# Moving TensorE's tiles in SBUF: operands on a line of 128 bytes, weights 64 bytes behind one

## The chip, the cores and the metric

The kernel runs on one core of a Trainium2 chip. The metric is the device time of one execution in microseconds (us), the median of several runs. SBUF is the on-chip memory that the engines read; a tile has 128 partitions, and a position in this document is a byte within a partition. "At 32" means 32 bytes behind a multiple of 128.

## The reference

One encoder layer on 1,024 tokens of 1,024 channels, all in float32:

```
h = x + 0.5 * SwiGLU_1(RMSNorm(x))                      # 1024 -> 2*2816 -> 1024
proj = RMSNorm(h) @ w_in                                # q, k, v, g_ret, p_pool, two gates (7 * 1024)
ret = retention(rotary(q), rotary(k), v)                # 4 heads of 256, chunks of 64, decay per head
ret = headnorm(ret) * silu(g_ret)
pool_out = (trailing means of windows 2/4/8/16 - token) @ pool_w * pool_scale
merged = sigmoid(gate0) * (ret @ w_ret_up) + sigmoid(gate1) * (pool_out @ w_pool_up)
h = h + merged @ w_out
h = h + 0.5 * SwiGLU_2(RMSNorm(h))
return RMSNorm(h)
```

Nearly all work is in the matrix products.

## The kernel before

Activations lie with channels on partitions and tokens along the row. Every float32 operand of a product is split into a high and a low float32r part (`split`, L150, and `split_scaled`, L154: ScalarE writes the high part, VectorE the rest), and `mm3` (L169) multiplies three times: high by high, high by low, low by high (L171 to L173). TensorE's instruction for one multiplication is a load of 128x128 weights and a stream of up to 512 moving columns; the load for the next one runs beside the stream.

The large products use Strassen's scheme (`strassen`, L415: seven products of blocks in place of eight), and some pairs of groups a second level of it with 256 columns (`common`, L521; it puts the blocks made by `blocks`, L337, into tiles of tags `tl` and `t4`). VectorE forms the sums and differences, and the low parts, of weights and operands. `values` (L1159) computes v with the roles swapped: the activations are the stationary operand and tiles of `wt` move. In the retention units (`Unit`, L1360) both operands are tiles of `mv`, except the masked scores `sm` (stationary, tag `t4`) and the running state (moving, tag `t4`). The end of the last stage (`turned`, L948) multiplies two operand tiles. `spread` (L224) multiplies by `ones_r`.

The order is written out by hand. `Flow.run` (L64) takes a list of steps, each a preparation (loads, weights) and a body (products); the preparation of a step comes four steps (`LOOK`) ahead of its body, and after each body one or two pieces of put-off VectorE and ScalarE work are taken from a queue. One step of a Strassen group is 4 x 3 multiplications. Nearly all DMAs are issued by SyncE (`load`, L133).

Tiles come from two pools in SBUF, `cp` and then `sb`. Within a pool tags are laid out in the order of their first request, each with its number of buffers, sizes rounded up to 32 bytes. Adding them up from the first free byte, 1,152 (itself a multiple of 128), gives:

| tiles | bytes of one x buffers | begins before (behind a multiple of 128) | after |
|---|---|---|---|
| vec, neg, cst | 256, 256, 1344 | 0, 0, 0 | same |
| warm, zero, ones_r | 32, 1024, 512 | 64, 96, 96 | same |
| `line` (new) | 32 | - | 96 |
| t4 (activations, results; sm, state), raw (weights as loaded) | 4096 x 9, 4096 x 4 | 96 | 0 |
| ss | 32 x 2 | 96 | 0 |
| wt (split weights) | 4096 x 5 | 32 | 64 |
| `between` (new) | 64 | - | 64 |
| mv (split operands), tl (loaded or spilled tiles) | 4096 x 28, 4096 x 4 | 32 | 0 |
| c2 (half tiles: sums, differences) | 2048 x 8 | 32 | 0 |

All slices that TensorE reads begin at multiples of 512 bytes within these tiles. Small tiles (roots, sums, edges) follow behind c2.

Of the kernel before, what the change touches and what calls it, by code (L numbers as in the profile page):

```python
# [10 lines left out]
F32 = mybir.dt.float32  # L11
F32R = mybir.dt.float32r
# [5 lines left out]
P = 128  # L18
# [31 lines left out]
N_MV, N_T4, N_RAW, N_WT, N_TL, N_C2 = 28, 9, 4, 5, 4, 8  # L50
# [39 lines left out]
def block_kernel(ctx: ExitStack, tc, x, x_tok, vecs, f1_in, f1_out, w_in, w_v, pool_w, w_ret, w_pool, w_o,  # L90
# [10 lines left out]
    cp = ctx.enter_context(tc.tile_pool(name="cp", bufs=1))  # L101
    sb = ctx.enter_context(tc.tile_pool(name="sb", bufs=1))
# [4 lines left out]
    def mv(name):  # L107
        return sb.tile([P, 2, H], F32R, tag="mv", bufs=N_MV, name=name)

    def wt(name):  # L110
        return sb.tile([P, 2, 4, P], F32R, tag="wt", bufs=N_WT, name=name)


    def raw(name):
# [48 lines left out]
    def weights(src, name):  # L163
        w = wt(name)
        n = src.shape[-1] // P
        split(flat(w, 0, n), flat(w, 1, n), src)
        return w
# [25 lines left out]
            mm(b, zero[:, :P], zero, start=True, stop=True)  # L193
    ident, ones = cst[:, C_ID : C_ID + P], cst[:, C_ONE : C_ONE + P]
    ones_r = cp.tile([P, P], F32R, name="ones_r")


    def inverse_root(sums, n, name):
# [1649 lines left out]
```

## Time and profile before

| | |
|---|---|
| time, median of 3 runs | 2164.43 us (2164.16 to 2165.67) |
| span of the profiled execution, first to last instruction | 2160.9 us |
| granted TensorE clock | 0.999 |
| TensorE busy with multiplications | 2148.0 us, 10,668 of them |
| VectorE busy | 1870.0 us |
| ScalarE busy | 1088.9 us |
| DMA | 320.92 MB, mean 149 GB/s |

The profiled execution has no time of its own beside its span; the median of the runs is 3.5 us above it. In the profile, "PE" is TensorE's multiplication, "PEld" its load of weights, "DVE" VectorE, "ACT" ScalarE, "SP" SyncE. A row of the timeline gives the start in us from the span's beginning, the length, engine, source line, operation, and written<-read tiles with their shape. Multiplications overlap in the records (a length of 0.39 us where the next starts much earlier), so the pace is read from the distance between starts.

### The profile page before, as it was taken

To read this page: it belongs to the slowest core of one execution; us is meant where nothing else is said; L and a number is where in the kernel's file an instruction comes from. 1 tells how busy PE (TensorE), PEld (TensorE's weight loads), DVE (VectorE), ACT (ScalarE), POOL (GpSimd) and SP (SyncE) were. 2 spreads that over 40 slices of the span, in tenths; PEclk is the share of its full clock that TensorE was granted. 3 is DMA by queue.
4 is the path that set the end of the run, shared out by engine and by line. 5 is a ranking of instruction groups with operands and counts; after the bars stand their busy time and mean duration, and the time that the engine had idled before them with its cause. 6 is when DMAs were issued, how large, how long until landed. Compare 5 with 4: busy or idle time off the path is not lost.

```text
span 2160.9 us, 29697 instructions
## 1 busy us (share of the span) xinstructions
PE 2148.0 (99%) x10668; PEld 1816.9 (84%) x10668; DVE 1870.0 (87%) x3300; ACT 1088.9 (50%) x2047; POOL 0.2 (0%) x4
## 2 busy tenths in 40 slices
PE   9999999999999999999999999999999999999998
PEld 7888888888888888888888898887888888888887
DVE  8799899998788798899767877899999989999784
ACT  8544444545656444444426754446644444455463
POOL 0000000000000000000000000000000000000000
PEclk9999999999999999999999999999999999999999
DMA  7232323596323333333485567624133232359532
GB/s 261 69 129 104 101 93 127 165 339 207 122 93 107 109 127 108 118 107 119 153 268 191 167 224 256 218 97 160 65 117 103 98 107 99 118 185 334 178 122 78
DMA packets 117828, 320.92 MB, mean 149 GB/s; under 512 B 12976, under 2 KB 17200, under 8 KB 117680
## 3 DMA queue, kind: packets, MB, share of 16 engines
q1 hardware_dynamic: 117104, 317.97, 43.4%
q8 instruction: 83, 1.36, 0.3%
q10 hardware_dynamic: 576, 1.05, 0.1%
q14 instruction: 65, 0.53, 0.1%
HBM read 228.27 MB, written 90.70 MB: 148 GB/s over the span
## 4 chain that ended last, share of the span: by engine, by line
PE 90%; DVE 7%; ACT 1%; issue 1%; DMA 1%; SPq 0%; ACTq 0%; DVEq 0%
PE c_b L171 2%; PE c_b L173 2%; PE c_b L172 2%; PE a_b L173 2%; PE a_b L171 2%; PE a_b L172 2%; PE c_e L173 2%; PE c_e L171 2%; PE c_e L172 2%; PE a_e L173 2%; PE a_e L171 1%; PE a_e L172 1%; PE bp6b L172 1%; PE bp6b L173 1%; PE bp6b L171 1%; PE c_a L172 1%
## 5 line engine op out<-in xcount | busy, mean ns | idle before, releaser
L172 PE MATMUL c_b<-n3T,c_wS 128*128 128x512 f32 x176 | 68.5, 389 | 0.0
L173 PE MATMUL c_b<-n3T,c_wS 128*128 128x512 f32 x176 | 68.5, 389 | 0.0
L171 PE MATMUL c_b<-n3T,c_wS 128*128 128x512 f32 x176 | 68.2, 390 | 0.0
L171 PE MATMUL a_b<-n1T,a_wS 128*128 128x512 f32 x168 | 65.5, 390 | 0.0
L172 PE MATMUL a_b<-n1T,a_wS 128*128 128x512 f32 x168 | 65.4, 389 | 0.0
L173 PE MATMUL a_b<-n1T,a_wS 128*128 128x512 f32 x168 | 65.4, 389 | 0.0
L173 PE MATMUL a_a<-n1R,a_wL 128*128 128x512 f32 x120 | 46.7, 390 | 0.8 <-DVE a_wL L152 0.8
L171 PE MATMUL a_a<-n1R,a_wL 128*128 128x512 f32 x120 | 46.8, 390 | 0.0
L172 PE MATMUL a_a<-n1R,a_wL 128*128 128x512 f32 x120 | 46.7, 389 | 0.0
L172 PE MATMUL c_a<-n3R,c_wL 128*128 128x512 f32 x112 | 43.7, 390 | 0.0
L171 PE MATMUL c_a<-n3R,c_wL 128*128 128x512 f32 x112 | 43.6, 389 | 0.0
L173 PE MATMUL c_a<-n3R,c_wL 128*128 128x512 f32 x112 | 43.6, 389 | 0.0
L173 PEld LDWEIGHTS c_b<-n3T,c_wS 128*128 128x128 f32 x176 | 33.0, 188 | 6.9
L171 PEld LDWEIGHTS c_b<-n3T,c_wS 128*128 128x128 f32 x176 | 33.0, 188 | 6.9
L172 PEld LDWEIGHTS c_b<-n3T,c_wS 128*128 128x128 f32 x176 | 33.0, 188 | 6.8
L171 PEld LDWEIGHTS a_b<-n1T,a_wS 128*128 128x128 f32 x168 | 31.5, 188 | 6.8 <-ACT a_v L471 0.3
L173 PEld LDWEIGHTS a_b<-n1T,a_wS 128*128 128x128 f32 x168 | 31.5, 188 | 6.6
L172 PEld LDWEIGHTS a_b<-n1T,a_wS 128*128 128x128 f32 x168 | 31.5, 188 | 6.5
L173 PE MATMUL c_e<-n3T,c_wS 128*128 128x512 f32 x88 | 35.1, 399 | 0.4 <-DVE c_wS L152 0.4
L171 PE MATMUL c_e<-n3T,c_wS 128*128 128x512 f32 x88 | 34.5, 393 | 0.0
L172 PE MATMUL c_e<-n3T,c_wS 128*128 128x512 f32 x88 | 34.4, 391 | 0.0
L173 PE MATMUL a_e<-n1T,a_wS 128*128 128x512 f32 x84 | 33.4, 398 | 0.9 <-DVE a_wS L152 0.9
(3058 smaller groups left out, 8076.2 us busy)
## 6 DMA issues: line engine op xcount, KB each, us to landing
c_ra<-in_f_in SPq DMA_DIRECT2D x22, 512.0 KB, 3.6
c_rb<-in_f_in SPq DMA_DIRECT2D x22, 512.0 KB, 4.1
a_ra<-in_f_in SPq DMA_DIRECT2D x21, 512.0 KB, 3.6
a_rb<-in_f_in SPq DMA_DIRECT2D x21, 512.0 KB, 4.4
t<-au SPq DMA_DIRECT2D x11, 512.0 KB, 2.6
b<-ag SPq DMA_DIRECT2D x11, 512.0 KB, 2.7
r<-au SPq DMA_DIRECT2D x11, 512.0 KB, 3.6
br<-r SPq DMA_DIRECT2D x11, 512.0 KB, 5.4
```

What stands on the lines that cost most here:

```text
L171: mm(dst, w[0], m[0], start=start, stop=False, skip_group_check=True)
L172: mm(dst, w[0], m[1], start=False, stop=False, skip_group_check=True)
L173: mm(dst, w[1], m[0], start=False, stop=stop, skip_group_check=True)
```

## The change

Two tiles are allocated that no instruction reads or writes. `line`, 32 bytes, stands at the end of the pool `cp`. `between`, 64 bytes, is requested once, right behind the first weights' tile, so that it lies behind the five buffers of `wt`. Everything allocated behind them moves up, as the table shows. No instruction, order, buffer count or shape changes.

```diff
+    between = []
+
     def wt(name):
-        return sb.tile([P, 2, 4, P], F32R, tag="wt", bufs=N_WT, name=name)
+
+        w = sb.tile([P, 2, 4, P], F32R, tag="wt", bufs=N_WT, name=name)
+        if not between:
+            between.append(sb.tile([P, 16], F32, tag="between", bufs=1, name="between"))
+        return w
...
     ones_r = cp.tile([P, P], F32R, name="ones_r")
+    cp.tile([P, 8], F32, name="line")
```

## Prediction

> **What bounds the kernel now.** I read the head of the page first (the span and the engines' shares), then TensorE's waits, then the chain of waits by engine.
>
> ```profile
> span 2160.9 us, 29697 instructions
> PE 2148.0 (99%) x10668; PEld 1816.9 (84%) x10668; DVE 1870.0 (87%) x3300; ACT 1088.9 (50%) x2047; POOL 0.2 (0%) x4
> PE set L193 <- DVE zero L188: 1.2, 1, 1.2
> PE a_e L173 <- DVE a_wS L152: 0.9, 2, 0.5
> PE 90%; DVE 7%; ACT 1%; issue 1%; DMA 1%; SPq 0%; ACTq 0%; DVEq 0%
> ```
>
> TensorE has 10,668 multiplications and is busy for 99%. Its longest waits are 1.2 and 0.9 us in total, and 90% of the chain is TensorE's own work. So the kernel is paced by how far apart two multiplications start, with VectorE (87%) close behind. A busy share says nothing of whether that distance is as short as it could be, so I measured it in the timeline, over stretches in which nothing waits. First, 512 columns, nine steps apart:
>
> ```profile
> 499.75 0.39 PE L171 MATMUL bp6b<-bp7m,bp7w 128*128 128x512 f32 x1
> ...
> 501.79 0.39 PE L171 MATMUL bp1a<-bp2m,bp2w 128*128 128x512 f32 x1
> ```
>
> 2.04 / 9 = 0.2267 us. Then 256 columns, where weights and moving operand both begin 32 bytes behind a line of 128 (13 steps), and 256 columns with the weights `sm` 96 behind and the moving `v` 32 behind (18 steps):
>
> ```profile
> 155.77 0.28 PE L171 MATMUL a_x<-n1R,a_wx 128*128 128x256 f32 x1
> ...
> 157.33 0.28 PE L172 MATMUL a_b<-n1R,a_wx 128*128 128x256 f32 x1
> 1183.66 0.28 PE L171 MATMUL ob<-v,sm 128*128 128x256 f32 x1
> ...
> 1185.70 0.28 PE L171 MATMUL xb<-state,q 128*128 128x256 f32 x1
> ```
>
> 1.56 / 13 = 0.1200 us and 2.04 / 18 = 0.1133 us. The same shape, the same engine, no waits, and 6% apart: the one thing that I find to differ systematically is where the tiles begin. That is the row on which this prediction rests.
>
> **What the change moves.** It adds no instruction, no wait and no transfer: two tiles that nobody writes, 32 and 64 bytes wide, shift what is allocated behind them. Positions are worked out from tile sizes and order of allocation (the section on the kernel has the table). Moving operands go from 32 (some from 96) to 0; the weights' tiles from 32 to 64, which is half a line from the moving operands. Tiles that VectorE, ScalarE and the DMA queues use go from 96 or 32 to 0.
>
> **Step 1: what a position costs.** 0.1200 − 0.1133 = 0.0067 us looks like a unit: 0.1200 is 18 of it, 0.1133 is 17, and 0.2267 is 34. Sixteen fp32 columns are 64 bytes, so 256 columns are 16 pieces of 64 bytes and 512 are 32. Beyond the pieces there are 2 units in 256 columns with equal positions, 1 with positions half a line apart, and 2 in 512 columns with equal positions. My reading: one unit because the operand begins inside a piece (32 bytes behind a 64-byte boundary) and touches one piece more, and one because the weights being loaded collide with it in the same half of a line. Both would go: 32 units = 0.2133 us for 512 columns, 0.1067 for 256. No row shows an fp32 product with the moving operand at 0 and the weights at 64; the bounds are 0.2133 (no unit left) and, above, the 0.230 that the last rival quotes. I take 0.2133, because the only steady rows half a line apart, those of 0.1133, lie on its side.
>
> A page bears on the size. The Trainium skill ("TensorE: Matmul & The Clock Gate", the section on 56 ns against 53.3 ns) gives 215.7 ns between warm multiplications of 512 columns, a fixed 2.5 ns above the bare columns. No row here shows it; by it some 19 us of the gain below would be lost (an estimate) and the sum would come to about 2084 us.
>
> For 256 columns the load of the weights may become the limit. Transposes, 128 columns with a load each, run at the load's pace:
>
> ```profile
> 2065.06 0.87 PE n4t L1674 x8
> ```
>
> 0.87 / 8 = 0.109 us, so I take 0.109 and not 0.1067.
>
> **Step 2: how many of each.** Counted over the program's multiplications, which match the 10,668 of the page's row one for one:
> - 512 columns, 32/32 before, half a line apart after (activations against weights' tiles, and the value projection where the roles are swapped): 7,896 × (0.2267 − 0.2133) = 105.3 us.
> - 512 columns, both in operand tiles and both at 0 after (the last stage's turned products): 132; one unit each, 0.9 us.
> - 256 columns, 32/32 before, half a line apart after: 1,578 × (0.1200 − 0.109) = 17.4 us.
> - 256 columns with the moving operand in a tile of tag t4, apart before and after: 228 × (0.1133 − 0.109) = 1.0 us.
> - 256 columns, both at 0 after (scores, state updates): 240, one unit each, 1.6 us. Products with `sm` or the state go from apart to equal: 288; one unit less for the start, one more for the collision, nothing.
> - Transposes, row sums, the products with `ones_r` (that tile lies ahead of the padding and stays at 96): nothing.
>
> Sum: 126 us of TensorE time, 5.8% of the span.
>
> **Step 3: what the other engines can follow.** VectorE's and ScalarE's own durations don't depend on the position: the source lies at 96 in the first, third and fifth row, at 32 in the second and fourth.
>
> ```profile
> L152 DVE TENSOR_TENSOR a_wL<-a_ra,a_wL 128x512 fp32r<-128x512 f32 x30 | 20.4, 683 | 3.6 <-ACT a_wL L151 3.6
> L152 DVE TENSOR_TENSOR a_wS<-a_S,a_wS 128x512 fp32r<-128x512 f32 x45 | 30.7, 685 | 4.0 <-ACT a_wS L151 4.0
> L716 DVE TENSOR_TENSOR au<-au,n1rb 128x512 f32<-128x512 f32 x44 | 29.9, 684 | 0.0
> L151 ACT CAST a_wS<-a_S 128x512 fp32r<-128x512 f32 x45 | 27.1, 620 | 13.3 <-PE a_a L173 5.0 <-DVE a_S L429 3.7 <-PE a_e L173 2.5
> L151 ACT CAST a_wL<-a_ra 128x512 fp32r<-128x512 f32 x30 | 18.4, 621 | 17.6 <-PE a_e L173 5.6 <-DVE ag L710 4.8 <-DMA a_ra<-in_f_in 2.6
> ```
>
> 683, 685 and 684 ns, and 620 and 621 ns: equal, so I cost them at nothing. The cover that TensorE gave VectorE shrinks, though, and this is where part of the gain stays. I cut the span into stretches and asked how long VectorE is busy in each (in a row: the stretch, its length, then busy time and, in brackets, instructions of TensorE, of its weight loads, of VectorE and of ScalarE):
>
> ```profile
> 27.00:54.00 27.00, 27.00 (x121) 22.36 (x120) 27.00 (x45) 25.52 (x48) 0.00 (x0) 1.00 0.59 194
> ...
> 162.00:189.00 27.00, 27.00 (x121) 22.36 (x120) 27.00 (x53) 13.12 (x24) 0.00 (x0) 1.00 0.33 116
> ...
> 594.00:621.00 27.00, 27.00 (x120) 22.34 (x120) 16.73 (x27) 9.98 (x18) 0.00 (x0) 1.00 0.33 95
> ...
> 1998.00:2025.00 27.00, 27.00 (x121) 22.36 (x120) 25.76 (x44) 13.57 (x24) 0.00 (x0) 1.00 0.60 200
> ```
>
> With 126 us less, TensorE would need 25.43 us for such a stretch. In 31 of the 80 (the first and the last stand above) VectorE is busy for longer; at 162 us it is busy for all of it, at 594 us for 16.73. The excess over 25.43 in those 31 adds up to 35 us, and that much cannot be gained unless work moves between stretches. How far it can move is open. With stretches of 54 us, 12 exceed and hold 19 us; with 13.5 us, 79 exceed and hold 49 us:
>
> ```profile
> 108.00:162.00 54.00, 52.51 (x264) 43.22 (x263) 52.65 (x99) 23.62 (x46) 0.00 (x0) 1.00 0.38 128
> ...
> 1944.00:1998.00 54.00, 54.00 (x240) 44.69 (x239) 51.52 (x86) 27.36 (x50) 0.00 (x0) 1.00 0.94 332
> 13.50:27.00 13.50, 13.50 (x62) 11.16 (x61) 13.05 (x21) 11.65 (x22) 0.00 (x0) 1.00 0.96 370
> ...
> 1998.00:2011.50 13.50, 13.50 (x61) 11.20 (x60) 13.50 (x24) 5.65 (x10) 0.00 (x0) 1.00 0.46 167
> ```
>
> The program prepares weights four steps ahead of their use and holds five weights' tiles; a step is some 12 multiplications, 2.7 us, so 11 to 14 us of lead, and the work put off in `flow` adds to that. I take 27 us, between the two. DMA moves alike (q1 below is 43.4% of the engines) and nothing waits on it for long; aligned destinations I cost at nothing, below nothing if transfers speed up, which no wait would pass on.
>
> ```profile
> q1 hardware_dynamic: 117104, 317.97, 43.4%
> ```
>
> **The sum.** 126 − 35 = 91 us. On the profiled execution: 2160.9 − 91 = 2070. The median of the three runs is 2164.43, 3.5 above that span, for what lies around it: 2164.4 − 91 = **2073 us**. With 19 or 49 us held back by VectorE it is 2057 or 2088. The runs lie within 0.07% of each other, so 0.2% (4.3 us) is what a measurement can tell.
>
> **The rivals.**
> - *Only the distance counts, not the start.* Each product half a line apart gains one unit: 7,896 × 0.0067 + 1,578 × 0.0067 = 63, and the 288 that become equal lose 1.9: 61 us, of which VectorE holds 12 by the same table (27 − 0.76 per stretch): 49, so 2115 us. For it: the only pairs of rows that differ, differ in distance; every row has a start 32 behind a 64-byte boundary, so the other half of my unit was never seen to vanish. Chance 0.16.
> - *512 columns have a fixed rate.* 34 units may be simply 17/16 of the columns, and the collision may show only where the load fills the whole time, at 256. Then 1,578 × 0.0067 − 1.9 = 8.6 us, little of it held: 2156 us. Chance 0.06.
> - *Nothing.* Either the unused tiles move nothing or positions don't matter: 2164 us. The Trainium skill ("SBUF — State Buffer", section on who interferes with whom) says that TensorE has two independent read ports and never waits on anyone. By that rule this is the outcome; the rows of 0.1200 and 0.1133 disagree with it. Chance 0.05.
> - *Slower: at 512 columns half a line apart is the worse position.* The only 512-column products that have it now are the 14 with `ones_r` (weights at 96, moving at 32):
>
> ```profile
> 83.19 0.62 PE L238 MATMUL n10b<-n10dg,ones_r 128*128 128x512 f32 x2
> ...
> 84.11 0.39 PE L171 MATMUL a_b<-n1R,a_wS 128*128 128x512 f32 x1
> 1557.45 0.62 PE L238 MATMUL n30b<-n30dg,ones_r 128*128 128x512 f32 x2
> ...
> 1557.91 0.40 PE L171 MATMUL c_b<-n3R,c_wS 128*128 128x512 f32 x1
> ```
>
> 0.92 / 4 and 0.46 / 2 are 0.230 us, above 0.2267. Spread over 7,896 that is +26 us, less the 8.6 at 256 columns: 2182 us. It decides as soon as a steady 512 goes above 0.2267 + 8.6 / 7,896 = 0.2278. Against it: these products stand alone, each between two changes of tile, and the ordinary one behind them is slow as well. Chance 0.15.
>
> **How the numbers follow.** The forecast has 0.58. Faster by over 0.2%: 0.58 + 0.16 + 0.06 = 0.80; within: 0.05; slower: 0.15. The forecast's own range is 2057 to 2088, stretched to 2050 for VectorE work that moves further than I think. For 8 in 10 the range must take in the distance, fixed-rate and no-change cases: up to 2166; the slower case and the edge of the first stay outside.
>
> **What would show it.** Right: steady starts about 0.2133 apart at 512 columns; about 0.109 at 256 against weights' tiles, 0.113 for scores; VectorE above 90% busy, with waits of TensorE for VectorE of some 35 us in the stretches above. Wrong: 0.220 (distance only), 0.2267 (fixed rate), 0.230 (worse), or 0.2133 reached and the gain far below 91 us (VectorE holds more than the table says).

## The result: slower by 0.6%, and the profile after

| | before | after |
|---|---|---|
| median, 4 runs each | 2164.53 us (2164.16 to 2165.67) | 2178.67 us (2176.16 to 2180.13) |
| ratio, 95% interval | 1 | 1.0063 (1.0051 to 1.0076) |
| span of the profiled execution | 2160.9 us | 2178.3 us |
| granted TensorE clock | 0.999 | 0.999 |

The kernel became 14 us slower; the forecast was 91 us faster. The head of the page after and its chain of waits by engine:

```profile
span 2178.3 us, 29697 instructions
PE 2163.9 (99%) x10668; PEld 1815.7 (83%) x10668; DVE 1872.5 (86%) x3300; ACT 1088.6 (50%) x2047; POOL 0.2 (0%) x4
PE 95%; DVE 3%; DMA 1%; ACT 1%; issue 0%; SPq 0%; DVEq 0%; ACTq 0%
```

The instructions are the same; TensorE's busy time rose by 15.9 us and its share of the chain from 90% to 95%. TensorE's longest waits after (total us, count, longest) are as short as before:

```profile
PE set L199 <- DVE zero L194: 1.2, 1, 1.2
PE c_x L177 <- DVE cg L570: 0.9, 1, 0.9
PE a_e L179 <- DVE a_wS L158: 0.8, 2, 0.5
```

So no new wait took the place of another. VectorE and ScalarE take as long for one instruction as before (groups by line, after; in each row the second number behind the bar is the mean in ns):

```profile
L158 DVE TENSOR_TENSOR a_wS<-a_S,a_wS 128x512 fp32r<-128x512 f32 x45 | 30.6, 682 | 5.5 <-ACT a_wS L157 5.5
L723 DVE TENSOR_TENSOR au<-au,n1rb 128x512 f32<-128x512 f32 x44 | 29.9, 683 | 0.0
L157 ACT CAST a_wS<-a_S 128x512 fp32r<-128x512 f32 x45 | 27.2, 621 | 13.1 <-PE a_a L179 5.3 <-DVE a_S L436 3.7 <-PE a_e L179 2.1
```

What is left is the pace of the multiplications. The timeline after, for the stretch shown of before (512 columns, nine steps), and then 20 steps of 256 columns against weights' tiles:

```profile
500.08 0.39 PE L177 MATMUL bp1a<-bp2m,bp2w 128*128 128x512 f32 x1
...
502.14 0.39 PE L177 MATMUL bp6b<-bp7m,bp7w 128*128 128x512 f32 x1
158.91 0.28 PE L177 MATMUL a_x<-n1R,a_wx 128*128 128x256 f32 x1
...
161.27 0.28 PE L179 MATMUL a_x<-n1R22y,a_ws 128*128 128x256 f32 x1
```

2.06 / 9 = 0.2289 us where it was 0.2267, and 2.36 / 20 = 0.1180 where it was 0.1200. The value projection, where activations are the stationary operand and the weights' tiles move, went further (before: 12 steps; after: 9):

```profile
1069.70 0.39 PE L171 MATMUL vL<-vL12w,n2R 128*128 128x512 f32 x1
...
1072.42 0.39 PE L171 MATMUL vL<-vL12w,n2R 128*128 128x512 f32 x1
1074.91 0.40 PE L177 MATMUL vL<-vL11w,n2R 128*128 128x512 f32 x1
...
1077.01 0.39 PE L177 MATMUL vL<-vL12w,n2R 128*128 128x512 f32 x1
```

2.72 / 12 = 0.2267 before, 2.10 / 9 = 0.2333 after. I added up the distances between starts over all products of both traces: products of 512 columns take 19.3 us more and those of 256 columns 1.7 us less; all starts together go from 2152.7 to 2170.1 us, which is the 17.4 by which the span grew. The loss is a slower pace of 512-column products. The spans differ by more than the medians (17.4 against 14.1 us) because the profiled execution after is the slowest of its four (2180.13 us), while that of before was quicker than any of its four: wherever a run lists both, its time is 1.8 us above its span, so 2160.9 us stands for about 2162.7 (an estimate from that).

One thing is left open by this: why 0.2333 in the value projection and 0.2289 elsewhere, though in both the two operands begin half a line of 128 bytes apart? Only the sign differs: weights minus moving operand is +64 bytes in the value projection and −64 elsewhere, which is 64 and 192 if positions are taken modulo 256.

### The profile page after: what moved, and what is told of

The parts are those of the page before. It is cut to its first block, busy times and chain, and to the rows that moved or that the text cites. A ratio compares the mean times of both kernels' runs of the same rounds, so it can differ in the third digit from the quotient of the medians.

```text
span 2178.3 us, 29697 instructions
## 1 busy us (share of the span) xinstructions
PE 2163.9 (99%) x10668; PEld 1815.7 (83%) x10668; DVE 1872.5 (86%) x3300; ACT 1088.6 (50%) x2047; POOL 0.2 (0%) x4
## 4 chain that ended last, share of the span: by engine, by line
PE 95%; DVE 3%; DMA 1%; ACT 1%; issue 0%; SPq 0%; DVEq 0%; ACTq 0%
PE c_b L177 2%; PE c_b L179 2%; PE c_b L178 2%; PE a_b L179 2%; PE a_b L177 2%; PE a_b L178 2%; PE c_e L179 2%; PE c_e L177 2%; PE c_e L178 2%; PE a_e L179 2%; PE a_e L177 2%; PE a_e L178 2%; PE a_a L179 1%; PE a_a L177 1%; PE c_a L177 1%; PE c_a L179 1%
## 5 line engine op out<-in xcount | busy, mean ns | idle before, releaser
L179 PE MATMUL c_e<-n3T,c_wS 128*128 128x512 f32 x88 | 35.2, 400 | 0.4 <-DVE c_wS L158 0.4
L158 DVE TENSOR_TENSOR a_wS<-a_S,a_wS 128x512 fp32r<-128x512 f32 x45 | 30.6, 682 | 5.5 <-ACT a_wS L157 5.5
L177 PE MATMUL c_e<-n3T,c_wS 128*128 128x512 f32 x88 | 34.7, 394 | 0.0
L177 PE MATMUL c_e<-n3T,c_wL 128*128 128x512 f32 x88 | 34.7, 394 | 0.0
```

The lines of the kernel that those rows point to most:

```text
L158: tt(lo, src, hi.bitcast(F32), SUB)
L177: mm(dst, w[0], m[0], start=start, stop=False, skip_group_check=True)
L179: mm(dst, w[1], m[0], start=False, stop=stop, skip_group_check=True)
```

## The experiments

"Distance" is the position of the weights minus that of the moving operand. Theory A is that only this distance sets the pace; A128 and A256 are its two forms later on, in which the distance counts modulo 128 or modulo 256 bytes. The rivals have the start of an operand on a line, or contention with the other engines' reads and writes, at work instead. Means in the text are over consecutive products of the same size and distance; distances over 245 ns (512 columns) or 126 ns (256 columns), which hold a wait, are left out.

**The two halves of the change, each alone.** The first adds only `line`, which moves starts from 32 to 64 (wt, mv, tl, c2) and from 96 to 0 (t4, raw) and keeps the distances; the second adds only `between`, which keeps starts off a line (wt 32, mv 96) and gives the distances of the change.

```diff
+    cp.tile([P, 8], F32, name="line")
```

> The 32 bytes at the end of the first pool alone: t4 and raw begin at 0 as in the changed kernel, wt, mv, tl and c2 all at 64, so weights and moving operands are again equal in position. Theory A (only the distance between weights and moving operand counts): 512 columns 0.2267 us apart, 256 columns 0.120, time as before, 2164 to 2166 us. Theory B (the loss comes from tiles that moved to a line, t4 and raw among them, through VectorE, ScalarE or the DMA queues): slower by a good part of the 14 us, 2170 or more. Theory C (my forecast's unit for a start inside a piece of 64 bytes): 64 is a boundary, so one unit of 0.0067 us less per product, over 2100 down to about 2110 us.

```diff
+        w = sb.tile([P, 2, 4, P], F32R, tag="wt", bufs=N_WT, name=name)
+        if not between:
+            between.append(sb.tile([P, 16], F32, tag="between", bufs=1, name="between"))
```

> The 64 bytes behind the weights' tiles alone: t4 and raw stay at 96, wt at 32, mv, tl and c2 go to 96; the distance between weights and moving operand is half a line, as in the changed kernel, and neither begins on a line of 128. Theory A (distance alone): the changed kernel's time, 2177 to 2181 us, 512 columns at 0.229 to 0.230 on the mean, 256 at 0.113 to 0.118. Theory B (loss from tiles that moved to a line): about 2164 us.

Measured: with `line` alone 2163.81 us, ratio to before 0.9997 (0.9988 to 1.0007); with `between` alone 2178.55 us, 1.0066 (1.0049 to 1.0083). Timeline of each, ten steps of 512 columns:

```profile
499.88 0.39 PE L172 MATMUL bp6b<-bp7m,bp7w 128*128 128x512 f32 x1
...
502.15 0.39 PE L173 MATMUL bp1a<-bp2m,bp2w 128*128 128x512 f32 x1
```

```profile
499.86 0.39 PE L178 MATMUL bp1a<-bp2m,bp2w 128*128 128x512 f32 x1
...
502.15 0.39 PE L179 MATMUL bp6b<-bp7m,bp7w 128*128 128x512 f32 x1
```

0.2270 with `line`, 0.2290 with `between`. The distance makes the whole loss and the start none of it, among the starts that these versions have (0, 32, 64 and 96).

**Everything on a line, nothing apart.** The change with `between` requested ahead of the weights' tile instead of behind it, so that all tiles that TensorE reads in the large products begin at 0 and the distance is 0.

```diff
         if not between:
             between.append(sb.tile([P, 16], F32, tag="between", bufs=1, name="between"))
+        return sb.tile([P, 2, 4, P], F32R, tag="wt", bufs=N_WT, name=name)
```

> The change with one thing turned round: the 64 bytes of between are requested ahead of the weights' tiles, not behind them, so that weights and moving operands all begin at 0, on the line of 128, as every other tile does. Theory A (distance alone): time of before, 2163 to 2166 us, 512 columns 0.2267 apart and 256 columns 0.120. If a start on the line is worth anything by itself, a time below 2160; if it costs, above 2168.

Measured: 2166.84 us, 1.0011 (1.0001 to 1.002). Ten steps in its timeline:

```profile
499.92 0.39 PE L176 MATMUL bp6b<-bp7m,bp7w 128*128 128x512 f32 x1
...
502.18 0.39 PE L177 MATMUL bp6b<-bp7m,bp7w 128*128 128x512 f32 x1
```

0.226 by these two rows, 227.0 ns in the mean of all; 256 columns at distance 0: 119.7 ns, the same as before (119.7). An aligned start buys nothing. The 0.1% that it lies above before fits the 256-column products of `sm`, the state and tag t4, which this edit moves from distances 64 and 192 (means 115.7 and 113.4 ns) to 128 (118.7): 330 × 3.0 + 136 × 5.3 ns = 1.7 us.

**Positions tried by themselves.** Ahead of the layer, rows of 24 products on one tile of tag t4, whose values are zero; `place` picks the start modulo 128, `n`, `m` and `w` in the names are columns, start of the moving operand and distance. The trials change two accumulators of the layer, so only their own rows count, not the time of 2289.78 us (one run). VectorE and ScalarE go on with the layer's preparations beside the first rows. From 42.1 us to the end of the trials at 132 us both are idle and the DMA queues move 1 GB/s, so the rows that start after 42.1 us ran alone.

```diff
+    def trial(name, n, weights, moving):
+        b = sum_bank(name)
+        for _ in range(24):
+            mm(b[:, :n], weights, moving, start=True, stop=True, skip_group_check=True)
...
+    for n in (512, 256):
+        for at in (0, 16, 32, 64):
+            for apart in range(0, 128, 16 if at == 0 else 64):
+                trial(f"n{n}m{at}w{apart}z", n, place(at + apart, P, 576), place(at, n))
```

> Ahead of the kernel, 30 rows of 24 products each on one tile that nothing else touches, so that no other engine's access can be the cause: bf16 512 columns at equal position and half a line apart; then fp32r of 512 and 256 columns with the moving operand at 0 (weights 0, 16, 32 up to 112 bytes further), and at 16, 32 and 64 (weights 0 and 64 further). These rows come on top of the layer's work (about 150 us) and the whole time says nothing. Theory A: fp32r 512 columns 0.2267 at distance 0 wherever the start, 0.229 to 0.236 at 64; 256 columns 0.120 at 0 and 0.113 to 0.118 at 64. Theory C: moving at 0 or 64 faster than at 16 or 32 by 0.0067. If the loss needs other engines' accesses: no difference between distances here. bf16: if the 6% above 0.2133 belong to fp32r, bf16 runs near 0.2160.

Timeline of the trials (each row is 24 products; from one row's start to the next, divided by 24, is the pace):

```profile
5.16 5.34 PE L205 MATMUL wb0z<-zero 128*128 128x512 bf16 x24
10.34 5.34 PE L205 MATMUL wb64z<-zero 128*128 128x512 bf16 x23
...
37.61 5.75 PE L205 MATMUL n512m0w64z<-zz 128*128 128x512 f32 x24
43.20 5.72 PE L205 MATMUL n512m0w80z<-zz 128*128 128x512 f32 x24
...
70.91 5.60 PE L205 MATMUL n512m32w0z<-zz 128*128 128x512 f32 x24
76.35 5.67 PE L205 MATMUL n512m32w64z<-zz 128*128 128x512 f32 x24
81.85 5.63 PE L205 MATMUL n512m64w0z<-zz 128*128 128x512 f32 x24
...
92.81 3.03 PE L205 MATMUL n256m0w0z<-zz 128*128 128x256 f32 x24
95.68 3.01 PE L205 MATMUL n256m0w16z<-zz 128*128 128x256 f32 x24
...
104.19 2.89 PE L205 MATMUL n256m0w64z<-zz 128*128 128x256 f32 x24
106.92 3.02 PE L205 MATMUL n256m0w80z<-zz 128*128 128x256 f32 x24
```

At 512 columns equal positions give 5.44 / 24 = 0.2267 (`n512m32w0z`), half a line apart 5.50 / 24 = 0.2292 (`n512m32w64z`) or 5.59 / 24 = 0.2329 (`n512m0w64z`). At 256 columns it is the other way round: 2.87 / 24 = 0.1196 for equal, 2.73 / 24 = 0.1137 for half a line. So the loss needs no other engine: `n512m32w0z` and `n512m32w64z` and all rows of 256 columns ran alone. `n512m0w64z` began while VectorE was busy, but its steps, 231 and 236 ns in turn, go on unchanged when VectorE stops at 42.1 us. The two bf16 rows have the same median step, 216 ns, at equal positions and half a line apart (one record of the second is missing). The two values for "half a line" are the 0.229 and 0.233 of the change again. In `n512m0w64z` the weights lie 64 behind the moving operand modulo 256, in `n512m32w64z` 192, because `place` wraps at 128; a reading modulo 128 does not separate them.

**All distances in the layer itself.** Before, with weights' tiles 128 bytes wider, and every 40 requests another offset of 0 to 112 bytes inside them.

```diff
-        return sb.tile([P, 2, 4, P], F32R, tag="wt", bufs=N_WT, name=name)
+        given.append(name)
+        o = 4 * (len(given) // 40 % 8)
+        w = sb.tile([P, 8 * P + 32], F32R, tag="wt", bufs=N_WT, name=name)
+        return w[:, o : o + 8 * P].rearrange("p (a b c) -> p a b c", a=2, b=4)
```

> Before, with 128 spare bytes in each weights' tile and the split weights put 0, 16, 32 up to 112 bytes behind the tile's start, changed every 40 weights' tiles: the same eight distances in the real work, moving operands at 32 throughout. Theory A: 512 columns 0.2267 at 0, slower at 64 (0.229 to 0.230), the others between or beyond; 256 columns the other way round. If a third distance is better than 0 at 512 columns, below 0.2267, a faster kernel is in reach. Time between before's and the changed kernel's, about 2164 to 2185 us.

Measured: 2197.79 us (one run), above the range expected. Sorted by distance modulo 128, as I first did, the products were disturbed even at 0: a buffer of 4,224 bytes is 33 × 128, so neighbouring buffers lie 128 bytes apart modulo 256. Sorted modulo 256 (512 columns, means in ns):

| distance | 0 | 16 | 32 | 48 | 64 | 80 | 96 | 112 |
|---|---|---|---|---|---|---|---|---|
| ns | 227.9 | 231.2 | 233.3 | 233.1 | 233.3 | 231.8 | 234.0 | 233.3 |
| distance | 128 | 144 | 160 | 176 | 192 | 208 | 224 | 240 |
| ns | 232.8 | 231.5 | 233.4 | 230.1 | 229.9 | 232.1 | 233.3 | 227.5 |

No distance is below 227. At 192, that of the change, 229.9; at 64, that of its value projection, 233.3. At two distances the trials differ from the layer: 16 had 227.0 there and has 231.2 here, 240 had 229.1 and has 227.5. The moving operand begins at 0 in the one and at 32 in the other, so distance alone does not settle the pace in steps of 16 bytes; why is open.

**Apart at 256 columns only.** Equal positions are best at 512 columns and distances of 64 and 192 at 256, so, starting from the version with everything on a line, the weights of `common` alone were moved by 64 bytes, in a weights' tile made 128 bytes wider.

```diff
+        w = sb.tile([P, 8 * P + 32], F32R, tag="wt", bufs=N_WT, name=name)
+        return w[:, o : o + 8 * P].rearrange("p (a b c) -> p a b c", a=2, b=4)
...
-            w["x"] = weights(a[src], f"{A.name}wx{n}")
+            w["x"] = weights(a[src], f"{A.name}wx{n}", 16)
```

> Everything on the line, distance 0, except the weights of the second-level products of 256 columns, which are put 64 bytes further in their tile (1,806 products). Theory A: 512 columns stay at 0.2267 where they run steadily, those 256 columns fall from 0.120 to between 0.1134 (as in the trial) and 0.117 (as in the changed kernel): 5 to 12 us less, 2153 to 2160 us. Against it: each change between the two distances may disturb the 512-column products behind it, at up to 0.005 us each; then 2160 to 2166 us.

Measured: 2188.24 us, 1.0109 (1.0092 to 1.0126): slower, where no product of 512 columns had been moved modulo 128. Its timeline shows why, 23 steps and then 11:

```profile
502.05 0.39 PE L177 MATMUL bp1a<-bp2m,bp2w 128*128 128x512 f32 x1
...
507.26 0.40 PE L179 MATMUL bp6b<-bp7m,bp7w 128*128 128x512 f32 x1
...
509.82 0.39 PE L178 MATMUL bp1a<-bp2m,bp2w 128*128 128x512 f32 x1
```

5.21 / 23 = 0.2265 and then 2.56 / 11 = 0.2327: the pace changes with the weights' buffer. Of its 8,028 products of 512 columns 4,800 lie at distance 128 modulo 256, with a mean of 232.6, and 3,228 at 0, with 227.9. This is where the period of 128 bytes, on which the prediction rested, fell; the next two runs put it to the test.

**A distance of 128, and one of 64.** First, before with `between` of 128 bytes and no `line`: modulo 128 nothing moves. Second, the change with 192 bytes in place of 64: modulo 128 it is the change.

```diff
-            between.append(sb.tile([P, 16], F32, tag="between", bufs=1, name="between"))
+            between.append(sb.tile([P, 32], F32, tag="between", bufs=1, name="between"))
```

> Before, with 128 bytes behind the weights' tiles and nothing else: t4 and raw at 96, wt at 32, mv, tl and c2 at 32 again, so that positions behind a line of 128 are all as in before. Theory A128 (what counts is the distance modulo 128): before's time, 2163 to 2167 us. Theory A256 (the distance counts modulo 256, as the two halves of the products of e6 suggest: 227.9 ns at distance 0 and 232.6 at 128): 7,896 products of 512 columns go from 0.2270 to about 0.2326, +44 us, 1,578 of 256 columns from 0.1197 to 0.1188, -1 us: 2207 us.

```diff
-            between.append(sb.tile([P, 16], F32, tag="between", bufs=1, name="between"))
+            between.append(sb.tile([P, 48], F32, tag="between", bufs=1, name="between"))
```

> The change with 192 in place of 64 bytes behind the weights' tiles: again wt at 64 and every other operand tile at 0 behind a line of 128, as the change says, but weights 64 bytes ahead of the moving operands modulo 256 and not 192. Theory A128: the changed kernel's time, 2177 to 2181 us. Theory A256: 7,560 products of 512 columns at the rate of distance 64, 0.2333 (seen for the 336 of the value projection) against 0.2270, +48 us; 1,806 of 256 columns from 0.1197 down to 0.1145 to 0.1164, -6 to -9 us: about 2205 us.

Measured: 2206.4 us, 1.0191 (1.0175 to 1.0207), and 2206.3 us, 1.0188 (1.0174 to 1.0202). Timeline of each, ten steps:

```profile
499.81 0.40 PE L178 MATMUL bp1a<-bp2m,bp2w 128*128 128x512 f32 x1
...
502.14 0.40 PE L179 MATMUL bp6b<-bp7m,bp7w 128*128 128x512 f32 x1
```

```profile
499.87 0.40 PE L178 MATMUL bp1a<-bp2m,bp2w 128*128 128x512 f32 x1
...
502.20 0.40 PE L179 MATMUL bp6b<-bp7m,bp7w 128*128 128x512 f32 x1
```

0.233 in both. With 128 bytes the operands keep their places modulo 128 and the kernel loses 42 us; with 192 in place of 64 the loss of the change triples, and its value projection, now at 192, falls from 233.3 to 228.9. Both times are within 1.5 us of what A256 gave (2207 and 2205) and far from those of A128. The period is 256 bytes, and not more: in the version before these two, products at 128 and at 384 modulo 512 both go 232.7 ns apart.

The Trainium skill ("SBUF — State Buffer", the section on who interferes with whom) says that TensorE has two independent read ports and never waits on anyone. By that, an unused tile of 128 bytes, with every instruction the same, should cost nothing; here it costs 42 us of TensorE's pace. The section is about what engines do to each other, and no other engine is needed for this loss. A conflict between TensorE's own two reads fits the rows, but the profile has no row of a port, so that stays an inference.

**What sets the floor of 0.2267.** Trials like the first, with other sizes: bf16, fewer weight columns (`c`), fewer moving columns (`n`).

```diff
+    for cols in (128, 64, 32):
+        for apart in (0, 64):
+            trial(f"c{cols}w{apart}z", 512, place(apart, cols, 576), place(0, 512))
+    for n in (448, 384, 320, 256, 192, 128):
+        for apart in (0, 64):
+            trial(f"n{n}w{apart}z", n, place(apart, P, 576), place(0, n))
```

> Trial rows ahead of the layer, 24 products each, moving operand at 0: bf16 of 512 columns; fp32r of 512 columns with weights of 128, 64 and 32 columns, at distance 0 and 64; then 128-column weights with 448 down to 128 moving columns at distances 0 and 64. The time as a whole says nothing. If the 0.0133 us above 0.2133 at 512 columns (and the further 0.003 at distance 64) come from the load of the weights colliding with the stream, both shrink with fewer weight columns, by about half at 64. If the 0.0133 is a rate of fp32r streams (17/16), it stays at 0.2267 for 64 and 32 weight columns and the steps are 0.1983 at 448, 0.1700 at 384, 0.1417 at 320 columns at distance 0; only what distance 64 adds shrinks.

```profile
22.58 5.69 PE L205 MATMUL c64w0z<-zz 128*64 128x512 f32 x24
28.11 5.75 PE L205 MATMUL c64w64z<-zz 128*64 128x512 f32 x24
33.69 5.72 PE L205 MATMUL c32w0z<-zz 128*32 128x512 f32 x24
39.25 5.72 PE L205 MATMUL c32w64z<-zz 128*32 128x512 f32 x24
...
66.47 3.68 PE L205 MATMUL n320w64z<-zz 128*128 128x320 f32 x24
69.99 3.04 PE L205 MATMUL n256w0z<-zz 128*128 128x256 f32 x24
72.86 2.99 PE L205 MATMUL n256w64z<-zz 128*128 128x256 f32 x24
75.69 2.82 PE L205 MATMUL n192w0z<-zz 128*128 128x192 f32 x24
```

3.52 / 24 = 0.1467 for 320 columns, 2.87 / 24 = 0.1196 for 256, 0.2267 for 512 (first trials): 64 columns more are 0.0267, and 0.0133 is left over at each of these sizes. At 384 and 448 columns, distance 0, it is somewhat more: steps of 0.1745 and 0.2030 leave 0.0145 and 0.0163. A rate of 17/16 would have given 0.1417 at 320 columns and is excluded. So the prediction's two "units" of 0.0067 beyond the bare columns are about 0.0133 per product, whatever its size, and neither positions (the sweep) nor fewer weight columns took it away at 512: 64 weight columns give 5.53 / 24 = 0.2304, 32 give 5.56 / 24 = 0.2317, no less than 128. (VectorE was busy beside these rows until 42 us; `c32w64z`, which runs past that, keeps its steps.) At 256 columns and distance 64 the step is 2.83 / 24 = 0.1179, where the same row of the first trials, with the same positions, had 0.1137: distance alone does not fix the pace of this size. The bf16 products of the first trials, at equal positions, go 5.18 / 24 = 0.2158 apart, which agrees with the 215.7 ns of the Trainium skill ("TensorE: Matmul & The Clock Gate", the section on 56 ns against 53.3 ns); the page's figure does not hold for the products of this kernel. What makes the 0.0133 is open.

**Apart at 256 columns, done rightly.** Before, with weights' tiles 256 bytes wider, so that all buffers keep their place modulo 256, and `common`'s weights 64 bytes further; `zero` moves into another tile to make room.

```diff
+        w = sb.tile([P, 8 * P + 64], F32R, tag="wt", bufs=N_WT, name=name)
+        return w[:, o : o + 8 * P].rearrange("p (a b c) -> p a b c", a=2, b=4)
...
+            w["x"] = weights(a[src], f"{A.name}wx{n}", 16)
...
+    zero = sb.tile([P, H], BF16, tag="dec", bufs=1, name="zero")
```

> e6 again with its flaw taken out: the spare bytes in each weights' tile are 256 and not 128, so that all five buffers have the same position modulo 256 (room for it: the tile of zeros used at the start shares the buffer of the decay tables). Products of 512 columns at distance 0; 1,578 second-level products of 256 columns at distance 64, 228 others with their moving operand in t4 go from 64 to 128. Theory A256: 512 columns 0.2270, those 256 columns 0.1197 to 0.1145 (-8.2 us), the 228 +0.7 us: 2155 to 2160 us, faster than both kernels. If changing between two distances disturbs the 512 columns behind, 2160 to 2168 us.

Measured: 2163.4 us, 0.9995 (0.9986 to 1.0003): no difference that can be told. 512 columns stay at 227.0. Of 256 columns 23 steps in its timeline, and its TensorE waits:

```profile
156.61 0.28 PE L172 MATMUL a_x<-n1R,a_wx 128*128 128x256 f32 x1
...
159.32 0.28 PE L174 MATMUL a_x<-n1R22y,a_ws 128*128 128x256 f32 x1
PE c_x L172 <- DVE cg L564: 1.2, 1, 1.2
PE a_x L172 <- DVE ag L564: 1.0, 1, 1.0
```

2.71 / 23 = 0.1178, where the trials had 0.1137 and the flawed version above a mean of 0.1145 at the same distance. The products of tag t4, now at 128, rose from 0.1152 to 0.1201. By these means 1,578 products gain 2 ns each and 228 lose 5, some 2 us in all, which the interval of the ratio can't tell from nothing. No version clearly beats the kernel before.

## Why the prediction was wrong, point by point

- **What bounds the kernel** held: TensorE's pace sets the end, no wait took over, and a change of 1% in that pace came out one for one in the span (17.4 us of starts, 17.4 us of span).
- **Step 1 failed, and it decided.** The term 7,896 × (0.2267 − 0.2133), 105.3 us of gain, became 19.3 us of loss. Its unit for "begins inside a piece" of 64 bytes does not exist: with all starts at 0 (everything on a line) 512 columns stay at 227.0 and 256 at 119.7. What I read as two units is the 0.0133 that every product has at distance 0. Its unit for the collision was real at 256 columns (119.7 ns at distance 0, 113.4 to 117.8 at 64 and 192), but I carried its sign over to 512, where it is the opposite: 227.0 at distance 0, 229.2 at 192, 233.3 at 64. The rows with `ones_r` at 0.230 were the only direct evidence at 512, and I set them aside because "these products stand alone", in favour of 0.2133, a value that no row showed. They lay at distance 192 modulo 256, the one that the change gave to 7,560 products.
- **Step 2's counts were right, its classes were not.** Modulo 256 the 7,896 products "half a line apart" are 7,560 at distance 192 and 336 at 64, with different prices, and the 288 products that I had as "equal" are at 128, at 118.9 ns. Modulo 128 also hid that before has 372 products of 256 columns at 64 and 144 at 192.
- **At 256 columns** I took 0.109, the load's pace; measured are 117.2 ns against weights' tiles, down from 119.7. 0.1133 is not a price of distance 192 alone: before's 136 at 192 have 113.4, the change's 1,517 at 192 have 117.2.
- **Step 3 was never tested.** TensorE did not get faster, so VectorE was not asked to hold anything back; its durations are unchanged, as predicted (682 and 683 ns). By its own terms the range that the step gives ends at 2087 and not at 2088.
- **The rivals.** "Only the distance counts, not the start" named the mechanism and had the wrong sign where it matters. "512 columns have a fixed rate" holds only at distance 0. "Nothing" is excluded by the interval of the ratio. "Slower" was the case that came: 2182 forecast, 2178.7 measured. Its terms were less exact than its sum: +26 at 512 columns came out as +19.3, because most go 0.2292 and not 0.230 apart, and −8.6 at 256 as −1.7. That the two errors cancel is luck.

The step at fault is thus a price taken from one size (256 columns) and used at another (512), against the only rows at that size.

## What to carry to other kernels

Where TensorE's pace bounds a kernel and float32r operands stream, read the distance between starts, and sort it by the position of weights minus moving operand modulo 256 bytes; here no distance was better than equal positions at 512 columns, and padding that shifts one tag against another by other than a multiple of 256 bytes, an unused tile or a wider buffer, moved the pace by up to 2.8% (227.0 to 233.3 ns). Take the price of a position only from rows of the same size, and give the few rows that speak against a forecast more weight than a tidy arithmetic of units. A buffer whose size is an odd multiple of 128 bytes puts every second buffer at another position.

## What the runs showed of the hardware that I had not expected

- Period 256 bytes: an unused tile of 128 bytes makes the kernel 1.91% slower (2206.4 us).
- A float32r product takes 0.0133 us more than its columns at 256, 320 and 512 columns alike (equal positions, or 64 apart for 320), and 0.0145 and 0.0163 at 384 and 448; a bf16 product of 512 columns has 0.2158, 2.5 ns more than 512 columns at the 0.0267 for 64 (0.2133).
- The same pair settles at different paces: 256 columns at distance 64 go 0.1137 apart in one set of trials, 0.1179 in the other, and 0.1178 in the last version's layer. What chooses between them is open.
- A moving start of 16 bytes breaks the pattern: at distance 0 the trial's mean is 231.1 ns, at 64 it is 229.0, the reverse in order of what starts at 32 and 0 show (226.7 at distance 0, 233.1 at 64). It was not followed up, since no tile of the layer begins there.
